# The last projection of a two-block transformer layer in seven half-size products instead of eight

## Chip, cores and metric

The kernel runs on one core of a Trainium2 chip. The metric is the device time of one execution in microseconds (us); the kernel is compared by the median of several executions. TensorE is called PE below, VectorE DVE, ScalarE ACT, GpSimd POOL, and SP is the queue that issues nearly all DMAs.

## What is computed

The reference is a sequence of two mixer blocks over 2048 tokens of width 1024, in float32. Only the end of the second block matters here:

```python
def swa_sink_mixer(xn, w_in, sinks, w_out, t5_table):
    q, k, v, z = split(xn @ w_in)
    o = banded_attention(q, k, v, t5_table, SWA_WINDOW, sinks)     # 16 heads, window 128
    return (merge_heads(o) * silu(z)) @ w_out                       # [2048,1024] @ [1024,1024]

x = x + swa_sink_mixer(rms_norm_2(x, norm_g), ...)
return rms_norm_2(x, final_g)
```

## The kernel before

The kernel is written as phases A, B1, B2, C, D and E, each a function that opens its own tile pools. Phase D computes the attention of the second block and stores its gated result, token tile by token tile, in DRAM as `y2[t]` (1024 x 128, already transposed for use as the stationary operand). Phase E, `phase_e`, is the last projection with the residual and the final norm: it loads `y2[t]` and `x2[t]` for each of 16 token tiles of 128, multiplies by `w_out`, adds the residual, and scales by the reciprocal root mean square and a gain.

Precision comes from splitting. Each float32 operand is cut into a high part (ACT copies it to the matmul type) and a low part (DVE or POOL subtracts the high part from the original), and `mm3` (L804 to L807) runs three matmuls for one 128-deep step: high by high, low by high, high by low. A token tile by half of the columns (512) is thus 8 steps of 3 matmuls; a token tile is 48 matmuls of 512 columns, and the phase 768 (the last tile's second half is cut in two, so 744 of 512 columns and 48 of 256).

A scheduler of the framework turns the program into one fixed order of instructions for each engine. Program order gives the priority; an instruction is placed once its inputs are there and its buffer is free, so a later phase may run in the gaps of an earlier one. Phase D's last stretch works in blocks `n` of one token tile and four heads: `scores(n)` (PE, then a fused add and max on DVE, L1115, then exponentials on ACT, L1120, and a scaling on POOL, L1128) and, two blocks later, `values(n-2)` (transposes, a high and low split on ACT and DVE, L1146 and L1147, matmuls, a copy on ACT, L1154, an addition on DVE, L1159, a product with the gate `e_z` on POOL, L1161, and the store to `y2`, L1162).

Memory decides when phase E may begin. Pools are laid out one behind another in the order in which they are opened. Phases D and E start from the same base, so each pool of E lies over certain pools of D. In KB per partition from that base, worked out from the shapes and buffer counts:

| pools of phase D | KB | pools of phase E before | KB |
|---|---|---|---|
| e_r (raw weights) | 0 to 8 | f_r | 0 to 4 |
| e_w0, e_w1 (split weights) | 8 to 40, 40 to 48 | f_w0, f_yr | 4 to 36, 36 to 40 |
| e_b (bias of the scores) | 48 to 56 | f_x0 | 40 to 48 |
| e_t (copies, outputs) | 56 to 63 | f_g (gain) | 48 to 52 |
| e_p (split probabilities) | 63 to 75 | f_x1 (7 buffers) | 52 to 80 |
| e_kv, e_s | 75 to 79.75 | f_s | 80 to 81.25 |
| e_a0, e_a1 (input x) | 79.75 to 131.75 | f_w1, f_y, f_j | 81.25 to 131.25 |
| e_q (queries) | 131.75 to 147.75 | f_x2 | 131.25 to 139.25 |
| e_z (gates), e_v (values) | 147.75 to 157.75, to 171.75 | | |
| e_k (keys), e_e (scores) | 171.75 to 187.75, to 203.75 | | |

In PSUM, phase D uses the eight banks as e_pm (0 to 2, projections), e_ps (3 and 4, scores), e_pt (5 and 6, transposes) and e_po (7, values). Phase E's one PSUM pool, `f_pm`, has three buffers and lies over e_pm. In the loop over tiles, `XN = 11` picks which of the three pools holds the tile of `x2`.

Of the kernel before, what the change touches and what calls it, by code (L numbers as in the profile page):

```python
# [7 lines left out]
F32 = mybir.dt.float32  # L8
F32R = mybir.dt.float32r
I32 = mybir.dt.int32  # L10
AF = mybir.ActivationFunctionType
ALU = mybir.AluOpType
AX = mybir.AxisListType
PSUM = bass.MemoryType.PSUM
DRAM = bass.MemoryType.DRAM

P = 128
S = 2048
D = 1024
NT = S // P  # L20
KD = D // P
# [782 lines left out]
def mm3(nc, ps, ah, al, bh, bl, first, last):  # L804
    nc.tensor.matmul(ps, ah, bh, start=first, stop=False)  # L805
    nc.tensor.matmul(ps, al, bh, start=False, stop=False)  # L806
    nc.tensor.matmul(ps, ah, bl, start=False, stop=last)  # L807
# [394 lines left out]
            pend = pend[per:]  # L1202


XN = 11


def phase_e(tc, c, scr, a_w_out, final_g, out):
    nc = tc.nc
    with (  # L1210
        tc.tile_pool(name="f_r", bufs=2) as rp,
        tc.tile_pool(name="f_w0", bufs=1) as wp0,
        tc.tile_pool(name="f_yr", bufs=1) as yrp,
        tc.tile_pool(name="f_x0", bufs=2) as xp0,
        tc.tile_pool(name="f_g", bufs=1) as gp,
        tc.tile_pool(name="f_x1", bufs=7) as xp1,
        tc.tile_pool(name="f_s", bufs=8) as sp,
        tc.tile_pool(name="f_w1", bufs=1) as wp1,
        tc.tile_pool(name="f_y", bufs=2) as yp,
        tc.tile_pool(name="f_j", bufs=1) as jp,  # L1220
        tc.tile_pool(name="f_x2", bufs=2) as xp2,
        tc.tile_pool(name="f_pm", bufs=3, space=PSUM) as pm,
    ):
        fg = gp.tile([P, D], F32, name="f_fg")
        nc.sync.dma_start(fg, final_g.unsqueeze(0).broadcast_to([P, D]))
        w = {}

        def load_w(ch, k):
            raw = rp.tile([P, 512], F32, name="f_raw")
            nc.sync.dma_start(raw, a_w_out[0, k * P:(k + 1) * P, ch * 512:(ch + 1) * 512])  # L1230
            t = (wp0, wp1)[ch].tile([P, 2, 512], F32R, name=f"f_w{ch}{k}")
            nc.scalar.activation(t[:, 0], raw, AF.Copy)
            nc.vector.tensor_sub(t[:, 1], raw, t[:, 0].bitcast(F32))
            w[ch, k] = t

        def load_y(t):
            yr = yrp.tile([P, KD, P], F32, name="f_yr")
            nc.sync.dma_start(yr, scr["y2"][t].rearrange("(k p) q -> p k q", p=P))
            y = yp.tile([P, 2, KD, P], F32R, name="f_y")
            nc.scalar.activation(y[:, 0], yr, AF.Copy)  # L1240
            nc.gpsimd.tensor_sub(y[:, 1], yr, y[:, 0].bitcast(F32))  # L1241
            return y

        ys = {0: load_y(0)}
        for ch in range(2):
            for k in range(KD):
                load_w(ch, k)
        for t in range(NT):
            if t + 1 < NT:
                ys[t + 1] = load_y(t + 1)  # L1250
            y = ys.pop(t)
            xt = (xp0, xp2, xp1)[min(t % XN // 2, 2)].tile([P, D], F32, name="f_xt")
            nc.sync.dma_start(xt, scr["x2"][t])  # L1253
            cuts = (0, 512, 1024) if t < NT - 1 else (0, 512, 768, 1024)
            sqs = []
            for a, b in zip(cuts, cuts[1:]):
                ch, ws = a // 512, slice(a % 512, a % 512 + b - a)
                ps = pm.tile([P, 512], F32, name="f_mm")[:, :b - a]
                for k in range(KD):
                    mm3(nc, ps, y[:, 0, k], y[:, 1, k], w[ch, k][:, 0, ws], w[ch, k][:, 1, ws], k == 0, k == KD - 1)  # L1260
                nc.vector.tensor_add(xt[:, a:b], ps, xt[:, a:b])  # L1261
                junk = jp.tile([P, 512], F32, name="f_j")
                sqs.append(sp.tile([P, 1], F32, name="f_sq"))
                nc.scalar.activation(junk[:, :b - a], xt[:, a:b], AF.Square, accum_out=sqs[-1])  # L1264
            ss = sqs[0]
            for sq in sqs[1:]:
                nc.vector.tensor_add(ss, ss, sq)
            rs = rsqrt_dve(nc, sp, ss, D)
            for a, b in ((0, D),) if t < NT - 1 else ((0, 512), (512, D)):
                nc.vector.scalar_tensor_tensor(xt[:, a:b], xt[:, a:b], rs, fg[:, a:b], ALU.mult, ALU.mult)  # L1270
                nc.sync.dma_start(out[0, t * P:(t + 1) * P, a:b], xt[:, a:b])


LAM_INIT = 0.8 - 0.6
# [101 lines left out]
```

## Time and profile before

| what | us |
|---|---|
| median of 3 runs | 3001.12 (2995.64 to 3003.31) |
| the profiled execution, its own time | 2997.43 |
| its span, first to last instruction | 2995.7 |

The span is the time from the first to the last instruction in the trace; the 1.7 us between it and the time lie around it. Times in the trace are counted from the span's start. A PE matmul of 512 columns shows 389 ns because matmuls are pipelined and overlap; the pace is read from starts, not from durations. A line number names the line of the kernel that issued an instruction.

### The profile page before, as it was taken

Reading aid. Unit: us, or ns where it says so; the run is one execution under the profiler, and the core shown is the slowest. Engines: PE = TensorE matmul, PEld = TensorE weight load, DVE = VectorE, ACT = ScalarE, POOL = GpSimd, SP = SyncE. Lnnn points to the kernel's source line nnn. Section 1 sums busy time; section 2 is a strip of 40 time slices with the busy share of each in tenths; the row PEclk is TensorE's granted clock in tenths of the full one; section 3 lists DMA queues with packets and bytes.
Section 4 is the critical chain, followed back from the end, with each engine's and each line's share of the span. In section 5 each row is a group of like instructions: output and inputs, shape, how many; then the busy total and the mean of one; then the engine's idle time right before and its main releaser. Section 6 shows DMA issues by size and latency. Waiting matters only on the chain. (4 is left out here: it accounts for less than half of the span.)

```text
span 2995.7 us, 45163 instructions
## 1 busy us (share of the span) xinstructions
PE 2893.5 (97%) x15554; PEld 2464.0 (82%) x15554; DVE 1802.1 (60%) x4607; ACT 1563.9 (52%) x3480; POOL 1240.7 (41%) x1156
## 2 busy tenths in 40 slices
PE   9999999999999999988898799999999999999998
PEld 7778888888788888888788678888788888888787
DVE  4115666522788889877666654444535756766765
ACT  5222333311588888878787642222345666666621
POOL 1110111100688888855676610000145565555421
PEclk9999999999999999999899999999999999999999
DMA  6653444414223322148666542332554343332452
GB/s 211 118 155 85 120 114 119 112 65 142 91 55 91 79 64 76 46 111 175 121 147 122 139 149 79 111 96 89 183 162 153 99 133 107 105 113 70 143 192 78
DMA packets 410646, 346.00 MB, mean 115 GB/s; under 512 B 89745, under 2 KB 356401, under 8 KB 408497
## 3 DMA queue, kind: packets, MB, share of 16 engines
q1 hardware_dynamic: 388000, 329.24, 39.3%
q10 hardware_dynamic: 20736, 8.65, 1.6%
q0 software_dynamic: 1680, 5.21, 0.7%
q8 instruction: 124, 2.03, 0.3%
q14 instruction: 106, 0.86, 0.1%
HBM read 227.51 MB, written 116.52 MB: 115 GB/s over the span
## 5 line engine op out<-in xcount | busy, mean ns | idle before, releaser
L190 PE MATMUL psm<-w,hh 128*128 128x512 f32 x1024 | 406.1, 398 | 9.4 <-DVE t L111 7.9
L191 PE MATMUL psm<-w,hl 128*128 128x512 f32 x1024 | 399.9, 392 | 0.0
L192 PE MATMUL psm<-w,hh 128*128 128x512 f32 x1024 | 399.8, 393 | 0.0
L101 POOL TENSOR_TENSOR w<-wraw,w 128x512 fp32r<-128x512 f32 x64 | 81.6, 1295 | 598.9 <-ACT w L100 596.3
L365 POOL TENSOR_TENSOR et<-et 128x1024 f32<-128x1024 f32 x124 | 296.3, 2414 | 0.0
L331 PE MATMUL s_ps<-kst,qst 128*128 128x512 f32 x1024 | 290.5, 408 | 4.1 <-DVE mx L337 3.1
L347 ACT ACTIVATE et<-et,nm 128x2048 f32<-128x2048 f32 x128 | 257.2, 2010 | 5.2
L1027 POOL TENSOR_TENSOR e_wt<-e_raw,e_wt 128x1024 fp32r<-128x1024 f32 x80 | 191.2, 2396 | 112.6 <-ACT e_wt L1026 111.4
L190 PEld LDWEIGHTS psm<-w,hh 128*128 128x128 f32 x1024 | 193.5, 189 | 48.1 <-DVE t L111 8.3
L805 PE MATMUL e_mm<-e_x,e_wt 128*128 128x512 f32 x576 | 228.1, 396 | 1.9 <-DVE e_k L1069 1.7
L807 PE MATMUL e_mm<-e_x,e_wt 128*128 128x512 f32 x576 | 226.8, 394 | 0.0
L192 PEld LDWEIGHTS psm<-w,hh 128*128 128x128 f32 x1024 | 193.2, 189 | 40.8
L806 PE MATMUL e_mm<-e_x,e_wt 128*128 128x512 f32 x576 | 226.6, 393 | 0.0
L191 PEld LDWEIGHTS psm<-w,hl 128*128 128x128 f32 x1024 | 193.7, 189 | 38.2
L331 PEld LDWEIGHTS s_ps<-kst,qst 128*128 128x128 f32 x1024 | 177.0, 191 | 43.7 <-DVE mx L337 17.3
L1128 POOL TENSOR_SCALAR e_es<-e_es,e_l 128x256 f32<-128x256 f32 (+1 forms) x256 | 118.8, 483 | 170.2 <-DVE e_l L1126 101.6
L364 POOL TENSOR_SCALAR et<-et,cc 128x1024 f32<-128x1024 f32 x124 | 138.3, 1132 | 110.4 <-PE psm L192 57.1
L377 DVE TENSOR_TENSOR ptl<-t_ps,pth 128x512 fp32r<-128x512 f32 x256 | 169.3, 684 | 18.9 <-ACT pth L376 18.4
L337 DVE CUSTOM_DVE_ANT_0 et<-s_ps,nd,mx 128x1024 f32<-128x1024 f32 x128 | 163.8, 1280 | 26.8 <-PE s_ps L331 24.9
L1115 DVE CUSTOM_DVE_ANT_0 e_es<-e_s,e_bias,e_sk 128x256 f32<-128x256 f32 (+1 forms) x256 | 117.3, 472 | 103.6 <-PE e_s L1107 72.1
L376 ACT ACTIVATE pth<-t_ps 128x512 fp32r<-128x512 f32 x256 | 143.6, 595 | 42.9 <-PE t_ps L375 38.9
L851 POOL TENSOR_TENSOR c_yn<-c_yn,ssq_sub 128x512 f32<-128x512 f32 x16 | 18.2, 1140 | 355.5 <-DMA c_yn<-s_y 327.5
(268 smaller groups left out, 7866.6 us busy)
## 6 DMA issues: line engine op xcount, KB each, us to landing
e_raw<-in_a_w_in_dram SPq DMA_DIRECT2D x80, 512.0 KB, 3.6
wraw<-in_w_in_dram SPq DMA_DIRECT2D x64, 256.0 KB, 3.5
kst<-s_dk SPq DMA_DIRECT2D x128, 128.0 KB, 3.9
s_xt<-c_at SPq DMA_DIRECT2D x32, 512.0 KB, 6.7
e_x<-s_xt SPq DMA_DIRECT2D x32, 512.0 KB, 7.9
t<-in_x_dram SPq DMA_DIRECT2D x32, 256.0 KB, 5.5
s_dv<-t SPq DMA_DIRECT2D x32, 256.0 KB, 3.0
s_bv<-t SPq DMA_DIRECT2D x32, 256.0 KB, 3.7
```

The lines of the kernel that those rows point to most:

```text
L190: nc.tensor.matmul(ps, ah, cur[k][:, 0], start=k == 0, stop=False)
L191: nc.tensor.matmul(ps, al, cur[k][:, 0], start=False, stop=False)
L192: nc.tensor.matmul(ps, ah, cur[k][:, 1], start=False, stop=k == KD - 1)
L331: nc.tensor.matmul(ps[:, b * 512:b * 512 + 512], lhs, heads[h, "k", e, i, 2 * hf + b], start=i == 0, stop=i == 1)
L337: nc.vector.tensor_tensor_reduce(et[:, hf], ps, bias[:, off:off + 1024], 1.0, -3.0e38 if hf == 0 else mx[:, 0:1], ALU.add, ALU.max, mx[:, ...
L347: nc.scalar.activation(ev, ev, AF.Exp, bias=nm, scale=slope, accum_out=st[g]["l"][:, e:e + 1])
L365: nc.gpsimd.tensor_sub(es[0][:, hf], es[0][:, hf], es[1][:, hf])
L377: nc.vector.tensor_sub(tl[:, :, qi], pt, th[:, :, qi].bitcast(F32))
L805: nc.tensor.matmul(ps, ah, bh, start=first, stop=False)
L806: nc.tensor.matmul(ps, al, bh, start=False, stop=False)
L807: nc.tensor.matmul(ps, ah, bl, start=False, stop=last)
L1027: nc.gpsimd.tensor_sub(w[:, 1], raw, w[:, 0].bitcast(F32))
```

## The change

`phase_e` is written anew. It takes two token tiles at once and cuts the product of the pair in two by two by two: two token tiles, two halves of the inner width (each 4 steps of 128), two halves of the columns. Eight half products become seven (Winograd's form of Strassen's scheme), each 4 steps of 3 matmuls of 512 columns, over these operands: a0 by w00, s2 by t2, s1 by t1, s3 by t3, s4 by w11, a1 by w10, b1 by t4. The weight combinations t1 to t4 are formed once (`weights`), the activation combinations s1 to s4 for each pair (`steps` in `load_pair`), each split anew into high and low. Seven weight operands of 4 tiles stand in place of 16 tiles. After each product its sum goes to the residual tiles `xa` and `xb` by way of a temporary `u` (ACT, DVE and POOL). The pools are new, too, in this order from the same base: `f_t` 0 to 32 KB (16 temporaries), `f_w0` 32 to 48 (w00), `f_x` 48 to 64 (x2), `f_g` 64 to 70, `f_s` 70 to 71.7, `f_w1` 71.7 to 135.7 (t1, t2, w10, t4), `f_y` 135.7 to 167.7 (8 split operands y), `f_w2` 167.7 to 199.7 (t3, w11). `f_pm` has seven PSUM buffers, banks 0 to 6. The last two tiles, not the last alone, are scaled and stored in halves. The new lines (removed ones, printed above, and empty ones are left out):

```diff
--- before.py
+++ after.py
@@ -1202,73 +1202,191 @@
             pend = pend[per:]
...
 def phase_e(tc, c, scr, a_w_out, final_g, out):
     nc = tc.nc
+    H = KD // 2
     with (
...
+        tc.tile_pool(name="f_t", bufs=TMP) as tp,
         tc.tile_pool(name="f_w0", bufs=1) as wp0,
...
+        tc.tile_pool(name="f_x", bufs=4) as xp,
         tc.tile_pool(name="f_g", bufs=1) as gp,
...
+        tc.tile_pool(name="f_s", bufs=6) as sp,
         tc.tile_pool(name="f_w1", bufs=1) as wp1,
...
+        tc.tile_pool(name="f_y", bufs=8) as yp,
+        tc.tile_pool(name="f_w2", bufs=1) as wp2,
+        tc.tile_pool(name="f_pm", bufs=7, space=PSUM) as pm,
     ):
+        def tmp():
+            return tp.tile([P, 512], F32, name="f_tmp", tag="f_tmp")
+        w = {}
+        def load_w(i, j, k):
+            raw = tmp()
+            nc.sync.dma_start(raw, a_w_out[0, (H * i + k) * P:(H * i + k + 1) * P, j * 512:(j + 1) * 512])
+            return raw
+        def split(key, k, raw, lo):
+            pool = wp0 if key == "w00" else wp2 if key in ("t3", "w11") else wp1
+            t = pool.tile([P, 2, 512], F32R, name=f"f_{key}_{k}")
+            nc.scalar.activation(t[:, 0], raw, AF.Copy)
+            lo.tensor_sub(t[:, 1], raw, t[:, 0].bitcast(F32))
+            w[key, k] = t
+        def weights():
+            ks = range(H)
+            w00 = [load_w(0, 0, k) for k in ks]
+            w01 = [load_w(0, 1, k) for k in ks]
+            for k in ks:
+                split("w00", k, w00[k], nc.vector)
+            for k in ks:
+                nc.gpsimd.tensor_sub(w00[k], w01[k], w00[k])
+            t1 = w00
+            w11 = [load_w(1, 1, k) for k in ks]
+            for k in ks:
+                split("t1", k, t1[k], nc.vector)
+            for k in ks:
+                nc.vector.tensor_sub(t1[k], w11[k], t1[k])
+                split("t2", k, t1[k], nc.vector)
+            t2 = t1
+            for k in ks:
+                nc.gpsimd.tensor_sub(w01[k], w11[k], w01[k])
+                split("t3", k, w01[k], nc.gpsimd if k % 2 else nc.vector)
+            for k in ks:
+                split("w11", k, w11[k], nc.gpsimd if k % 2 else nc.vector)
+            w10 = []
+            for k in ks:
+                w10.append(load_w(1, 0, k))
+                split("w10", k, w10[k], nc.gpsimd if k % 2 else nc.vector)
+            for k in ks:
+                nc.gpsimd.tensor_sub(t2[k], w10[k], t2[k])
+                split("t4", k, t2[k], nc.gpsimd if k % 2 else nc.vector)
+        ops, xs = {}, {}
+        def load_pair(n):
+            raw = {}
+            for i in range(2):
+                src = scr["y2"][2 * n + i].rearrange("(k p) q -> p k q", p=P)
+                for j in range(2):
+                    raw[i, j] = tmp()
+                    nc.sync.dma_start(raw[i, j].rearrange("p (k q) -> p k q", q=P), src[:, H * j:H * j + H])
+            def y_op(key, t, lo):
+                o = yp.tile([P, 2, H, P], F32R, name="f_y", tag="f_y")
+                tv = t.rearrange("p (k q) -> p k q", q=P)
+                nc.scalar.activation(o[:, 0], tv, AF.Copy)
+                lo.tensor_sub(o[:, 1], tv, o[:, 0].bitcast(F32))
+                ops[n, key] = o
+            def steps():
+                y_op("a0", raw[0, 0], nc.vector)
+                s1 = tmp()
+                nc.gpsimd.tensor_add(s1, raw[1, 0], raw[1, 1])
+                s2 = tmp()
+                nc.gpsimd.tensor_sub(s2, s1, raw[0, 0])
+                yield
+                y_op("s2", s2, nc.vector)
+                yield
+                y_op("s1", s1, nc.vector)
+                yield
+                nc.gpsimd.tensor_sub(raw[0, 0], raw[0, 0], raw[1, 0])
+                y_op("s3", raw[0, 0], nc.gpsimd)
+                yield
+                nc.gpsimd.tensor_sub(s2, raw[0, 1], s2)
+                y_op("s4", s2, nc.gpsimd)
+                yield
+                y_op("a1", raw[0, 1], nc.gpsimd)
+                yield
+                y_op("b1", raw[1, 1], nc.vector)
+                yield
+            xs[n] = []
+            for i in range(2):
+                xt = xp.tile([P, D], F32, name="f_xt")
+                nc.sync.dma_start(xt, scr["x2"][2 * n + i])
+                xs[n].append(xt)
+            return steps()
+        def product(n, ykey, wkey):
+            y = ops.pop((n, ykey))
+            ps = pm.tile([P, 512], F32, name="f_mm")
+            for k in range(H):
+                t = w[wkey, k]
+                mm3(nc, ps, y[:, 0, k], y[:, 1, k], t[:, 0], t[:, 1], k == 0, k == H - 1)
+            return ps
+        def add(x, j, ps):
+            nc.vector.tensor_add(x[:, 512 * j:512 * j + 512], ps, x[:, 512 * j:512 * j + 512])
+        def square(x, j, acc):
+            junk = gp.tile([P, 512], F32, name="f_j")
+            nc.scalar.activation(junk, x[:, 512 * j:512 * j + 512], AF.Square, accum_out=acc)
+        def finish(t, x, sq):
+            ss = sp.tile([P, 1], F32, name="f_ss")
+            nc.vector.tensor_scalar(ss, sq[0], sq[1], None, ALU.add)
+            rs = rsqrt_dve(nc, sp, ss, D)
+            for a, b in ((0, D),) if t < NT - 2 else ((0, 512), (512, D)):
+                nc.vector.scalar_tensor_tensor(x[:, a:b], x[:, a:b], rs, fg[:, a:b], ALU.mult, ALU.mult)
+                nc.sync.dma_start(out[0, t * P:(t + 1) * P, a:b], x[:, a:b])
+        first = load_pair(0)
+        for _ in range(2):
+            next(first)
+        weights()
+        for _ in first:
+            pass
         fg = gp.tile([P, D], F32, name="f_fg")
         nc.sync.dma_start(fg, final_g.unsqueeze(0).broadcast_to([P, D]))
...
+        for n in range(NT // 2):
+            nxt = load_pair(n + 1) if n + 1 < NT // 2 else iter(())
+            xa, xb = xs.pop(n)
+            sq = [[sp.tile([P, 1], F32, name=f"f_sq{i}{j}") for j in range(2)] for i in range(2)]
+            p = product(n, "a0", "w00")
+            u = tmp()
+            nc.scalar.activation(u, p, AF.Copy)
+            nc.gpsimd.tensor_add(xa[:, 0:512], xa[:, 0:512], u)
+            next(nxt, None)
+            p = product(n, "s2", "t2")
+            nc.vector.tensor_add(u, p, u)
+            nc.gpsimd.tensor_add(xa[:, 512:D], xa[:, 512:D], u)
+            next(nxt, None)
+            p = product(n, "s1", "t1")
+            add(xa, 1, p)
+            add(xb, 1, p)
+            next(nxt, None)
+            p = product(n, "s3", "t3")
+            nc.vector.tensor_add(u, p, u)
+            for j in range(2):
+                nc.gpsimd.tensor_add(xb[:, 512 * j:512 * j + 512], xb[:, 512 * j:512 * j + 512], u)
+            next(nxt, None)
+            p = product(n, "s4", "w11")
+            add(xa, 1, p)
+            square(xa, 1, sq[0][1])
+            square(xb, 1, sq[1][1])
+            next(nxt, None)
+            p = product(n, "a1", "w10")
+            add(xa, 0, p)
+            square(xa, 0, sq[0][0])
+            finish(2 * n, xa, sq[0])
+            next(nxt, None)
+            p = product(n, "b1", "t4")
+            add(xb, 0, p)
+            square(xb, 0, sq[1][0])
+            for _ in nxt:
+                pass
+            finish(2 * n + 1, xb, sq[1])
+TMP = 16
 LAM_INIT = 0.8 - 0.6
```

## Rows read from the trace of the kernel before

**Rows 1.** The page: busy time, share of the span and instructions of each engine.

```profile
PE 2893.5 (97%) x15554; PEld 2464.0 (82%) x15554; DVE 1802.1 (60%) x4607; ACT 1563.9 (52%) x3480; POOL 1240.7 (41%) x1156
```

**Rows 2.** Busy time by stretch: length, engines, granted clock, DMA share, GB/s.

```profile
2780.00:2794.00 14.00, 10.88 (x55) 8.93 (x54) 10.03 (x33) 10.53 (x29) 5.47 (x7) 0.88 0.76 230
2794.00:2858.00 64.00, 63.32 (x318) 52.25 (x318) 52.76 (x142) 37.53 (x96) 30.70 (x44) 1.00 0.49 156
2858.00:2988.00 130.00, 129.46 (x593) 107.70 (x591) 73.06 (x170) 28.29 (x63) 26.33 (x11) 1.00 0.38 131
```

**Rows 3.** Tile f_mm, 2788 to 2857.6 us: durations ns min/median/max, first and last start.

```profile
L805 PE MATMUL f_mm<-f_w,f_y x67: 389/389/500, 2794.4 to 2857.5; 128*128 128x512 f32 x67
```

**Rows 4.** SP's queue in order of time: start, us, line and DMA.

```profile
2779.76 0.36 SPq L1238 DMA_DIRECT2D f_yr<-s_y  x1
...
2830.01 0.96 SPq L1253 DMA_DIRECT2D f_xt<-s_x  x2
2831.46 0.33 SPq L1225 DMA_DIRECT2D f_fg<-in_final_g_dram  x1
...
2857.57 0.37 SPq L1162 DMA_DIRECT2D s_y<-e_o  x1
2858.70 5.20 SPq L1253 DMA_DIRECT2D f_xt<-s_x  x8
...
2914.76 0.37 SPq L1238 DMA_DIRECT2D f_yr<-s_y  x1
...
2925.64 0.37 SPq L1238 DMA_DIRECT2D f_yr<-s_y  x1
```

**Rows 5.** Timeline of DVE and POOL, apart: last reads of phase D's pools.

```profile
2830.95 0.48 DVE L1115 CUSTOM_DVE_ANT_0 e_es<-e_s,e_bias,e_sk 128x256 f32<-128x256 f32 x1
...
2846.95 1.29 DVE L1147 TENSOR_TENSOR e_pl<-e_tp,e_ph 128x512 fp32r<-128x512 f32 x2
...
2856.67 0.88 POOL L1161 TENSOR_TENSOR e_o<-e_o,e_z 128x128 f32<-128x128 f32 x2 [4.44 <-DVE e_o L1159]
```

**Rows 6.** Groups by line and shape, 2779.7 to 2857.6 us: count, busy us, mean ns, idle before.

```profile
L1233 DVE TENSOR_TENSOR f_w<-f_raw,f_w 128x512 fp32r<-128x512 f32 x16 | 12.9, 817 | 2.4 <-ACT f_w L1232 2.2
L1115 DVE CUSTOM_DVE_ANT_0 e_es<-e_s,e_bias,e_sk 128x256 f32<-128x256 f32 x26 | 12.1, 476 | 3.9 <-PE e_s L1107 3.7
L1147 DVE TENSOR_TENSOR e_pl<-e_tp,e_ph 128x512 fp32r<-128x512 f32 x16 | 10.6, 684 | 0.3 <-ACT e_ph L1146 0.2
L1232 ACT ACTIVATE f_w<-f_raw 128x512 fp32r<-128x512 f32 x16 | 10.0, 628 | 9.1 <-DMA f_raw<-in_a_w_out_dram 7.1 <-issue 2.0
L1159 DVE TENSOR_TENSOR e_o<-e_o,e_tmpb 64x256 f32<-64x256 f32 x18 | 7.5, 414 | 1.8 <-ACT e_tmpb L1154 1.0 <-issue 0.7
```

**Rows 7.** Timeline of DVE and PE where no f_mm has begun.

```profile
2787.57 0.47 DVE L1115 CUSTOM_DVE_ANT_0 e_es<-e_s,e_bias,e_sk 128x256 f32<-128x256 f32 x1
...
2792.14 0.47 DVE L1115 CUSTOM_DVE_ANT_0 e_es<-e_s,e_bias,e_sk 128x256 f32<-128x256 f32 x1
...
2788.10 0.90 PE L1107 MATMUL e_s<-e_k,e_q 128*128 128x256 f32 x4 [2.64 <-DVE e_mx L1115]
```

**Rows 8.** Groups by line and shape, 2600 us to the end.

```profile
L1241 POOL TENSOR_TENSOR f_y<-f_yr,f_y 128x1024 fp32r<-128x1024 f32 x16 | 38.3, 2392 | 96.9 <-ACT f_y L1240 90.9 <-DVE e_mx L1115 6.1
L1261 DVE TENSOR_TENSOR f_xt<-f_mm,f_xt 128x512 f32<-128x512 f32 x31 | 21.0, 687 | 29.2 <-PE f_mm L807 28.7 <-DMA f_xt<-s_x 0.3
L1264 ACT ACTIVATE f_j<-f_xt 128x512 f32<-128x512 f32 x31 | 19.4, 625 | 78.2 <-DVE f_xt L1261 42.1 <-issue 29.6 <-DMA f_xt<-s_x 6.5
L1270 DVE SCALAR_TENSOR_TENSOR f_xt<-f_xt,rd_y,f_fg 128x1024 f32<-128x1024 f32 x15 | 19.3, 1285 | 2.7 <-DMA f_fg<-in_final_g_dram 2.2
```

**Rows 9.** Busy time by stretch, just after that idle time of PE.

```profile
2792.00:2796.00 4.00, 4.00 (x21) 3.57 (x20) 2.99 (x12) 3.95 (x11) 0.00 (x0) 0.76 0.25 74
```

**Rows 10.** Timeline of the end, from the last matmul.

```profile
2987.30 0.28 PE L807 MATMUL f_mm<-f_w,f_y 128*128 128x256 f32 x1
2987.62 0.42 DVE L1261 TENSOR_TENSOR f_xt<-f_mm,f_xt 128x256 f32<-128x256 f32 x1 [1.65 <-PE f_mm L807]
```

More of the change, by code (lines that the diff above doesn't have):

```diff
@@ L1202, in phase_d @@
             pend = pend[per:]
-XN = 11
 def phase_e(tc, c, scr, a_w_out, final_g, out):
     nc = tc.nc
+    H = KD // 2
     with (
-        tc.tile_pool(name="f_r", bufs=2) as rp,
+        tc.tile_pool(name="f_t", bufs=TMP) as tp,
         tc.tile_pool(name="f_w0", bufs=1) as wp0,
-        tc.tile_pool(name="f_yr", bufs=1) as yrp,
-        tc.tile_pool(name="f_x0", bufs=2) as xp0,
+        tc.tile_pool(name="f_x", bufs=4) as xp,
         tc.tile_pool(name="f_g", bufs=1) as gp,
-        tc.tile_pool(name="f_x1", bufs=7) as xp1,
-        tc.tile_pool(name="f_s", bufs=8) as sp,
+        tc.tile_pool(name="f_s", bufs=6) as sp,
@@ L1218, in phase_e @@
         tc.tile_pool(name="f_w1", bufs=1) as wp1,
[L1219 to L1222, printed above, removed]
-    ):
+        tc.tile_pool(name="f_y", bufs=8) as yp,
+        tc.tile_pool(name="f_w2", bufs=1) as wp2,
+        tc.tile_pool(name="f_pm", bufs=7, space=PSUM) as pm,
+    ):
+        def tmp():
[105 more added lines that the diff above has]
+            pass
@@ L1224, in phase_e @@
         fg = gp.tile([P, D], F32, name="f_fg")
         nc.sync.dma_start(fg, final_g.unsqueeze(0).broadcast_to([P, D]))
[L1226 to L1271, printed above, removed]
```

## The prediction

> **What bounds the kernel now.** I read the page first: PE is busy for 97% of the span and no other engine comes near [rows 1]. Then the stretches around phase E. From 2794 to 2988 us PE has no room: 63.3 of 64 us, then 129.5 of 130 [rows 2]. But these are two kinds of stretch. In the first, phase D still runs: its last product with the gate ends at 2857.55 [rows 5]. PE is full there only because matmuls of phase E fill the gaps: by 2857.5 it has run 199 of E's 792 (the row of one line, x67, stands; those of the two others have x66 each) [rows 3]. In the second PE runs phase E alone, one token tile every 10.88 us [rows 4], or 10.88 / 48 = 0.2267 us a matmul. So the 199 were worth 45.1 us of PE time that cost nothing. The last matmul ends at 2987.58 [rows 10], and 8.1 us later the span.
>
> The question is thus double: how many matmuls fewer, and how many can still run under D's tail. For the second I read SP's queue, since a DMA into a pool shows when the pool opens. The gain `f_fg` lies over the first half of e_b, and is issued at 2831.46, when the last read of any bias ends (2830.95 + 0.48) [rows 4, 5]. f_x1 lies over e_b to e_a0, and its first buffer (52 to 56 KB) over e_b's second half alone, free since 2831.4. Yet nothing is loaded into any of its seven buffers until the batch of eight loads at 2858.70, behind the last product on POOL and the last store from e_t [rows 4, 5]. So a pool waits for every pool under any part of it; no buffer opens by itself. f_yr opens at 2779.76 [rows 4], and f_mm, over e_pm alone, starts at 2794.4 [rows 3].
>
> **When the new pools open.** Laid against the table: f_t lies over e_r and e_w0 and opens at about 2780; f_w0 over e_w0 and e_w1, soon after. So raw loads, w00's split, s1, s2, and t1's and part of t3's raw differences can run under D. Nothing else can. f_pm with seven banks lies over the transposes, read last by L1147 at 2848.2 [rows 5]. f_w1 begins at 71.7 KB, inside e_p (63 to 75), and f_w2 lies over e_v, e_k and e_e: all these live until D's last matmuls. f_y lies over e_q, e_z and e_v, and e_z is read by the very last product, so it opens latest; f_x waits for e_t besides. Call the end of that last product T1. No matmul of phase E starts before T1: all 45.1 us of cover are gone.
>
> **What that does to T1.** With PE's gaps unfilled, D's tail can run faster. DVE's main work of D left at 2780 is 12.1 + 10.6 + 7.5 = 30.2 us [rows 6], and w00 adds 4 x 0.82 = 3.3. That puts T1 at 2814 at the earliest, and with the short operations and the last block's chain at 2820. The other bound is 2857.6, as before. Where no f_mm had begun, six heads of scores took 5 us, 2787.57 to 2792.61 [rows 7]; all 26 from 2780 to 2831.4 took 51 us [rows 5, 6], 2 us each against 0.84. So the tail is held by PE's order, not by DVE, and I take a value nearer the low end. Nine blocks of values are left (L1159 x18) [rows 6]; at 6 us each T1 = 2834. PE may run this at the lower clock: after 2.64 us of idle time the granted clock was 0.76 from 2792 to 2796 [rows 7, 9]; that is why I don't take 5 us a block.
>
> **The sum after T1.** First matmul: ACT's copy of a0 (0.63 [rows 6]), DVE's subtraction (0.7 to 0.8) and the hand-overs, 2.2 us. Matmuls: 7 x 12 x 8 = 672 at 0.2267 = 152.3 us. Before it was 45.1 + 130.0 = 175.1, so the scheme does save 22.8.
>
> Stalls of the first pair. A POOL subtraction of 512 columns is half of L1241's 2.39, 1.2 us [rows 8]. From about T1 - 2.9, when f_w1 and f_w2 open, POOL has 2 differences of t3, 8 low parts, 4 differences of t4 and 5 operations for s3, s4 and a1: 19 x 1.2 = 22.8 us. The 16 temporaries are all taken then (4 raw y, s1, s2, 4 of t1, 4 of w01, 2 of w11), so w11's last two and w10's four loads wait for one to be freed, and POOL waits for them, some 5 us in all. POOL would be through the pair at T1 + 25, and two products of 2.7 us still follow: T1 + 30, against T1 + 2.2 + 19.0 = 21.2 without stalls. The next pair waits 1 us more. Bounds: 0, if the scheduler puts s4 and a1 into POOL's early gaps, and 15, if DVE's list (20 weight operations, 4 low parts, 7 sums from PSUM, 20 us) comes on top in part. I take 9.5, as the list of POOL gives it. PE starts from little work, so 1.5 us for the lower clock [rows 9].
>
> Steady state costs nothing more. A pair is 84 matmuls, 19.0 us of PE. POOL has 11 operations, 13.2 us. DVE has 7 sums at 0.69, 4 low parts at 0.82, 2 scalings at 1.29 [rows 6, 8] and two chains of short operations under 3 us each, 16 us. ACT has 8 copies and 4 squares at 0.63, under 9. Each operand is made a pair ahead. If a pair took 1 us more on DVE, the cover would be gone and it would cost 7 us.
>
> Tail: 8.1 us before. The last sum and square are of 512 columns in place of 256, 0.5 more, and tile 14's finish, one product earlier, stands in front of them on DVE: 0 to 3 us, I take 0.9. So 9.5.
>
> Sum: 2834 + 2.2 + 152.3 + 9.5 + 1.5 + 9.5 = 3009.0. With the 1.7 us around the span 3010.7, against the profiled execution's 2997.43: 13.3 us slower. The median of the runs shown is 3.7 above that execution, so I add the difference to the median: 3014.
>
> **Rivals.** (a) D's tail shrinks to DVE's floor: T1 = 2820, and 14 us less, about 3000, no change. For it speak the six heads in 5 us; against it the chain of one block through five engines, and the lower clock. (b) The other side, faster: buffers open one by one and not with their pool. Then PSUM banks 0 to 2 are free at 2794, the products start under D as before, and the 22.8 us are kept less 1.4 of tail: 2980. It decides where the 45 us of cover are kept; for it only that f_mm starts early before, against it the eight loads at 2858.70 and f_fg. (c) D's tail does not shrink: T1 = 2857.6, 3038. Against it rows 7. (d) POOL and DVE shut each other out: a subtraction with both inputs in SBUF took 817 ns on the mean while POOL worked, one with PSUM 684 [rows 6]. If each of DVE's 24 such operations in the first pair blocked POOL for 0.69 us, POOL's 23 operations up to its last sum, 27.6 us, became 44, and the pair ended 10 us later: 3024. The rows show only 0.13 us each. The Trainium skill (SBUF — State Buffer, "Who interferes with whom") has a rule for this: a DVE operation with two SBUF inputs and a POOL operation that reads SBUF exclude each other for a whole instruction. By that rule the sum would be 3024; by the rows, 3014.
>
> **From these to the numbers.** 0.3%, 9 us, is about what a measurement of this kernel can tell from no change. The forecast has 0.57, with 3005 to 3023 as its own range, a sixth of it within 9 us of 3001; (a) 0.20; (b) 0.07; (c) 0.06; (d) 0.10. Slower: 0.57 x 5/6 + 0.06 + 0.10 and a little of (a), 0.65; same 0.28; faster (b), 0.07. The range leaves out (b), most of (c) and the corner of (a) with no stalls: 2997 to 3033.
>
> **What would show it.** The first f_mm starts 1 to 3 us after the last L1161 product of D, not near 2794, and PE is mostly idle from 2795 to T1. Loads into the `f_x` tiles come right after the last store to y2, in a batch. D's last product ends at 2826 to 2845. The first 84 f_mm take 25 to 33 us, with waits on POOL; later pairs 19.0 each. The prediction is wrong if f_mm start while D's scores run, if T1 is below 2822, or if the steady pair is not 19 us.

## The result: slower by 1.4%

The kernel with seven products takes 3040.36 us (median of 4, 3038.2 to 3043.81), the kernel before in the same rounds 3000.7: a ratio of 1.014, 95% interval 1.0126 to 1.0155, or 40 us slower. The prediction said 3014 and a range up to 3033: its direction came, its size did not. The profiled execution took 3042.17 us, its span 3040.4.

The page of the changed kernel, busy time and then the chain that ended last, by engine. PE's share has fallen from 97% to 95% [rows 1]; its busy time has not (2896.1 us against 2893.5), although it has 120 matmuls fewer. The largest part of the chain that ends last is DVE's.

```profile
PE 2896.1 (95%) x15434; PEld 2458.2 (81%) x15434; DVE 1870.5 (62%) x4670; ACT 1590.6 (52%) x3538; POOL 1354.9 (45%) x1248
...
DVE 4%; issue 1%; POOL 1%; DMA 1%; PE 0%; ACT 0%; POOLq 0%; DVEq 0%; SPq 0%; ACTq 0%
```

Where phase E begins: the last product of phase D on POOL, SP's queue around it, and two rows of the tile `f_mm` (first and last start of its matmuls).

```profile
2830.86 1.76 POOL L1161 TENSOR_TENSOR e_o<-e_o,e_z 128x128 f32<-128x128 f32 x2 [2.06 <-issue]
```

```profile
2829.28 0.42 SPq L1348 DMA_DIRECT2D f_fg<-in_final_g_dram  x1
2832.65 0.36 SPq L1162 DMA_DIRECT2D s_y<-e_o  x1
2834.58 1.28 SPq L1314 DMA_DIRECT2D f_xt<-s_x  x3
```

```profile
L805 PE MATMUL f_mm<-f_w,f_y x96: 387/389/796, 2834.5 to 3017.8; 128*128 128x512 f32 x96
...
L807 PE MATMUL f_mm<-f_t,f_y x128: 387/389/794, 2844.1 to 3021.0; 128*128 128x512 f32 x128
```

The product ends at 2832.6 (T1). Before, `f_mm` started at 2794.4, under phase D [rows 3]; now its first matmul comes at 2834.5, 1.9 us behind T1, and the `x2` loads come in a batch behind the last store. So far all is as predicted, but for one sign: PE is not mostly idle from 2795 to T1. From there the windows tell the rest (length, busy time of PE, PEld, DVE, ACT and POOL with counts, granted clock, DMA share, GB/s):

```profile
2844.50:2854.50 10.00, 6.51 (x26) 4.56 (x24) 10.00 (x7) 6.32 (x13) 10.00 (x7) 0.95 0.49 151
...
2894.50:2914.50 20.00, 20.00 (x90) 16.48 (x89) 18.87 (x37) 6.17 (x15) 14.62 (x10) 1.00 0.48 159
...
2954.50:2974.50 20.00, 17.56 (x78) 14.21 (x77) 15.19 (x34) 6.36 (x15) 13.93 (x10) 1.00 0.50 159
2974.50:2994.50 20.00, 17.11 (x68) 13.59 (x67) 15.21 (x27) 6.31 (x14) 14.01 (x11) 0.91 0.44 144
...
3021.20:3040.40 19.20, 0.21 (x1) 0.00 (x0) 12.65 (x34) 2.89 (x8) 3.72 (x3) 0.58 0.22 83
```

The first line is the one to read: DVE and POOL are both busy for all of 10 us, and each gets only seven operations done. Later PE is full for three pairs, then runs dry again, with DVE at 15 and POOL at 14 of 20 us. The last matmul ends at 3021.2 (its start at 3021.0 and the pace of 0.23), so the matmuls take 186.7 us from first to last, where 672 at 0.2267 are 152.3. Then come 19.2 us without PE, where before had 8.1 [rows 10]. Counted by the starts of its matmuls, 84 at a time, the 186.7 us are 32.6, 30.4, 19.1, 19.1, 19.1, 21.8, 23.9 and 20.6: the loss lies in the first two blocks and in the last three. (A block is not quite a pair: PE runs 12 matmuls of the second pair before the first pair's last, which ends at 2870.4.)

Why seven operations take 10 us is seen in the timelines of the two engines, DVE first, then POOL (start, us, operations merged by line):

```profile
2849.70 1.75 DVE L1240 TENSOR_TENSOR f_w<-f_tmp,f_w 128x512 fp32r<-128x512 f32 x1
2851.38 5.12 DVE L1240 TENSOR_TENSOR f_t<-f_tmp,f_t 128x512 fp32r<-128x512 f32 x3
2856.42 3.46 DVE L1240 TENSOR_TENSOR f_w<-f_tmp,f_w 128x512 fp32r<-128x512 f32 x2
```

```profile
2850.86 1.73 POOL L1240 TENSOR_TENSOR f_w<-f_tmp,f_w 128x512 fp32r<-128x512 f32 x1
2852.55 5.08 POOL L1269 TENSOR_TENSOR f_tmp<-f_tmp 128x512 f32<-128x512 f32 x3
2857.59 1.75 POOL L1240 TENSOR_TENSOR f_w<-f_tmp,f_w 128x512 fp32r<-128x512 f32 x1
```

Each engine finishes one subtraction every 1.7 us, in step with the other. An earlier one on DVE, at 2837.68, when POOL stood idle, took 0.68, and POOL's of this size take 1.26 to 1.31 alone. One behind the other they would take some 1.96 us, side by side 1.28: at 1.71 the two come near to taking turns. This is called the lock below. The turns need not be even. Here one low part on DVE lasts 5.46 us, while POOL runs four operations without a gap, and PE waits 5 us for it (timelines of DVE, POOL and PE):

```profile
2873.59 5.46 DVE L1286 TENSOR_TENSOR f_y<-f_tmp,f_y 128x512 fp32r<-128x512 f32 x1
```

```profile
2873.57 1.28 POOL L1292 TENSOR_TENSOR f_tmp<-f_tmp 128x512 f32<-128x512 f32 x1
2874.79 1.27 POOL L1300 TENSOR_TENSOR f_tmp<-f_tmp 128x512 f32<-128x512 f32 x1
2876.01 2.49 POOL L1369 TENSOR_TENSOR f_xt<-f_xt,f_tmp 128x512 f32<-128x512 f32 x2
```

```profile
2879.11 0.79 PE L806 MATMUL f_mm<-f_t,f_y 128*128 128x512 f32 x1 [4.99 <-DVE f_y L1286]
```

In the later pairs (groups of DVE, 2885 to 3021 us; count, busy us, mean ns, idle before):

```profile
L1338 DVE SCALAR_TENSOR_TENSOR f_xt<-f_xt,rd_y,f_fg 128x1024 f32<-128x1024 f32 x13 | 28.7, 2204 | 0.2
L1286 DVE TENSOR_TENSOR f_y<-f_tmp,f_y 128x512 fp32r<-128x512 f32 x25 | 27.7, 1124 | 21.0 <-ACT f_y L1285 21.0
L1327 DVE TENSOR_TENSOR f_xt<-f_mm,f_xt 128x512 f32<-128x512 f32 x30 | 19.5, 678 | 0.3 <-issue 0.3
```

The scaling, 1285 ns in before [rows 8], takes 2204; the low parts take 1124; the sums with one input in PSUM take 678 (687 before [rows 8]). The waits of 2880 to 3021 us, longest first in total, show the second half of it:

```profile
ACT f_y L1285 <- POOL f_tmp L1300: 30.7, 6, 7.3
DVE f_y L1286 <- ACT f_y L1285: 21.0, 6, 4.5
...
PE f_mm L806 <- DVE f_y L1286: 6.5, 3, 2.9
```

ACT stands behind a late POOL, DVE behind ACT, PE behind DVE: so DVE has idle time and is late all the same. By these waits alone POOL could be slow on its own account; the experiments e9 and e11 decide that.

### The profile page after: what moved, and what is told of

Read it like the earlier page. It is cut to its first block, busy times and chain, and to the rows that moved or that the text cites. A ratio compares the mean times of both kernels' runs of the same rounds, so it can differ in the third digit from the quotient of the medians.

```text
span 3040.4 us, 45276 instructions
## 1 busy us (share of the span) xinstructions
PE 2896.1 (95%) x15434; PEld 2458.2 (81%) x15434; DVE 1870.5 (62%) x4670; ACT 1590.6 (52%) x3538; POOL 1354.9 (45%) x1248
```

## The experiments

Phases ahead of E end up to 16 us apart from run to run (the last bias load is issued at 2764.1 before, 2766.1 after and up to 2779.7 below), and chips differ; each run below is compared with runs of the kernel before on its own chip, and terms are counted from T1 or the first `f_mm`. "Stretch" is first start to last end of `f_mm`, "tail" what follows.

**e1_before_7banks**: the kernel before, but no bank of `f_pm` is free under D's tail.

```diff
-        tc.tile_pool(name="f_pm", bufs=3, space=PSUM) as pm,
+        tc.tile_pool(name="f_pm", bufs=7, space=PSUM) as pm,
```

> The kernel before with one number changed: seven PSUM buffers in the pool of the last projection in place of three, so that it lies over the banks of the scores and the transposes too. Theory (a pool opens as a whole, when every pool under it is done): no matmul of the last projection starts at 2794 us any more; the first starts when the last transposed tile is read, some 2828 to 2835 us, D's tail ends near 2833 as in the changed kernel, and as weights and y are ready the 792 matmuls follow without a gap: 2830 + 175 + 8, a span of 3010 to 3016 us, 13 to 18 us slower than before. Rival (a buffer opens by itself, and the stalls of the changed kernel alone make it slow): first matmul near 2794 us and no change.

Measured: 3030.35 against 3008.26, ratio 1.007 (1.0055 to 1.0085), 22 us slower. T1 2849.9, first `f_mm` 2847.1, behind the last transposes; window of the stretch:

```profile
2847.00:3023.20 176.20, 176.20 (x793) 146.57 (x792) 95.53 (x215) 36.83 (x79) 34.41 (x16) 0.99 0.35 121
```

PE runs its 792 matmuls without a gap, all but the first 2.8 us of them behind D. So the loss of cover alone costs 22 us (13 to 18 were expected): about half of the 45 us that the matmuls are worth, since D's tail gets shorter: T1 comes 70.2 us behind the last bias load, where before it was 93.4.

**e2_waits_by_tile**: each of the nine pools declared with waits by tile.

```diff
-        tc.tile_pool(name="f_t", bufs=TMP) as tp,
+        tc.tile_pool(name="f_t", bufs=TMP, reuse_waits="tile") as tp,
...
```

> The changed kernel, with its nine pools told to wait buffer by buffer for what lies under each, and not as whole pools. Theory: PSUM banks 0 to 2 and some y buffers open under D's tail, so the first matmul of the projection starts between 2795 and 2815 us in place of 2834.5; but t1's first tile and t3's tiles still lie under buffers that D reads to its end, so only two to four products gain cover: 5 to 12 us faster than the changed kernel, 3028 to 3035 us. Rival (the start does not matter, the list of DVE and POOL does): within 4 us of 3040.

Measured: 3044.41, ratio 1.0125 (1.0108 to 1.0143). The option left the order of instructions on every engine as it was; the first `f_mm` came at 2839.4, 1.9 us behind T1 (2837.5). The expected gain is not there, and the run tells nothing of the theory.

**e3_weights_on_dve**: the 20 weight operations of POOL given to DVE.

```diff
-                split("t3", k, w01[k], nc.gpsimd if k % 2 else nc.vector)
+                split("t3", k, w01[k], nc.vector)
...
```

> The changed kernel, with the 20 POOL operations that form and split the weights moved to DVE. Theory (a DVE operation with two SBUF inputs and a POOL operation shut each other out: both ran at one per 1.71 us together from 2841 to 2865 us, against 0.6 to 0.69 and 1.28 alone): a weight operation costs DVE 0.6 to 0.7 us when POOL is quiet, the 1.71 us rhythm disappears for most of the start-up, and the first pair is through 8 to 14 us earlier: 3026 to 3033 us. Rival (DVE's list is simply long; its operations are slow for another reason): DVE's list grows from 24 to 44 operations and the first pair ends up to 10 us later, 3040 to 3050 us.

Measured: 3042.25 against 3008.26, ratio 1.011 (1.0095 to 1.0125). Stretch 177.0 us against 186.7, tail 17.5. DVE has 20 operations more and PE is 9.7 us earlier through, which speaks for the lock and against DVE's mere load. The gain is not where it was expected: the first 84 matmuls take 29.5 us for 32.6, the second 84 take 19.1 for 30.4, and later blocks lose some of it again (21.8, 23.9, 20.6 and 23.9 us among the last five).

**e4_direct_last_pair**: the last pair's sums go straight from PSUM into the residual.

```diff
+            last = n == NT // 2 - 1
...
+            if last:
+                for x in (xa, xb):
+                    for j in range(2):
+                        add(x, j, p)
...
```

> The changed kernel; in the last pair alone every product is added from PSUM straight to the residual tiles on DVE (14 additions), with no temporary u, no ACT copy and no POOL addition. Theory (the 19 us from the last matmul to the end are the chain of u through ACT, DVE and POOL): 11 to 13 us from the last matmul to the end, 6 to 8 us faster, about 3033 us. Rival (DVE is late with older work, the norm and scaling of the pair before): the end stays 17 to 20 us behind the last matmul, 3040 us, or more as DVE has 7 more operations.

Measured: 3049.6, ratio 1.0137 (1.0122 to 1.0152); stretch 186.3, tail 19.8. The chain through `u`, ACT and POOL is not what makes the tail long. That theory falls; the rival, older work on DVE, fits.

**e5_after_again**: the changed kernel once more, beside the next three.

> The changed kernel itself once more, as the base for the next three on one chip. Every theory: ratio to before 1.013 to 1.015, some 40 us slower; matmuls of phase E last 185 to 189 us and the tail behind them 18 to 20 us.

Measured: 3047.84 against 3005.61, ratio 1.0139 (1.0122 to 1.0157). Stretch 187.2, tail 16.3 (18 to 20 was expected; so the tail of one and the same kernel differs by 3 us between two profiles).

**e6_three_banks**: the changed kernel with three PSUM buffers in `f_pm`.

```diff
-        tc.tile_pool(name="f_pm", bufs=7, space=PSUM) as pm,
+        tc.tile_pool(name="f_pm", bufs=3, space=PSUM) as pm,
```

> f_pm has 3 PSUM buffers instead of 7. Theory (DVE is the bound of phase E, and PE only runs ahead of it by as many sums as there are buffers): the end stays within 4 us of the changed kernel, the matmul stretch grows by 6 to 12 us and the tail behind the last matmul shrinks by as much, to 8 to 13 us. Rival 1 (the tail of 19 us is a chain of its own, of norm, scaling and store): the tail stays at 17 to 20 us and the total grows by what PE waits more, 6 to 12 us. Rival 2 (PE's run-ahead is what keeps the pace): the stretch grows by 20 us or more.

Measured: 3050.07, ratio 1.0145 (1.0128 to 1.0162), 2 us over e5. Stretch 195.8, tail 10.4. Against e5 the tail loses 5.9 us and the stretch gains 8.6; PE's new wait is for the sums:

```profile
PE f_mm L805 <- DVE f_xt L1327: 12.2, 6, 3.1
```

So the long tail is not work at the end. It is lag: seven banks let PE run ahead of sums that are late anyway.

**e7_no_pool**: all of phase E's POOL work given to DVE.

```diff
-                nc.gpsimd.tensor_sub(w00[k], w01[k], w00[k])
+                nc.vector.tensor_sub(w00[k], w01[k], w00[k])
...
-                y_op("s3", raw[0, 0], nc.gpsimd)
+                y_op("s3", raw[0, 0], nc.vector)
...
-            nc.gpsimd.tensor_add(xa[:, 0:512], xa[:, 0:512], u)
+            nc.vector.tensor_add(xa[:, 0:512], xa[:, 0:512], u)
...
```

> All of phase E's POOL work is given to DVE: the weight operations and, in each pair, 4 combinations, 3 low parts and 4 additions into the residual. Theory (DVE's operations with two SBUF inputs and POOL's shut each other out): the 512-column operations on DVE fall to 0.60 to 0.70 us each from 1.1 to 1.7, the scaling of 1024 to 1.29 from 2.20, and DVE's list of a pair is 7 x 0.69 + 4 x 0.62 + 7 x 0.68 + 4 x 0.62 + 2 x 1.29 + short operations = 18 to 19.5 us, under PE's 19.0 or just at it: the matmul stretch shrinks from 187 to 160 to 172 us, the tail to 9 to 15 us, the total by 15 to 30 us. Rival (the loss is DVE's load as such, and POOL carries a real share of it): DVE has 11 more operations, 7 us, in each pair of 22 us, so the stretch grows by 10 to 40 us and the total with it.

Measured: 3017.62 against 3005.61, ratio 1.0043 (1.0026 to 1.0059): 30 us faster than e5. T1 2840.9, first `f_mm` 2842.8, stretch 162.8, tail 10.4. Groups of DVE, 2880 to 3000 us, and two windows:

```profile
L1286 DVE TENSOR_TENSOR f_y<-f_tmp,f_y 128x512 fp32r<-128x512 f32 x44 | 29.9, 696 | 2.5 <-ACT f_y L1285 2.5
...
L1338 DVE SCALAR_TENSOR_TENSOR f_xt<-f_xt,rd_y,f_fg 128x1024 f32<-128x1024 f32 x12 | 15.3, 1280 | 0.0
```

```profile
2862.80:2872.80 10.00, 7.80 (x34) 5.71 (x32) 10.00 (x17) 3.42 (x6) 0.00 (x0) 1.00 0.33 98
...
2942.80:2962.80 20.00, 19.92 (x88) 16.18 (x87) 18.87 (x37) 7.38 (x16) 0.00 (x0) 1.00 0.81 263
```

One engine does the work of two in less time: 17 operations in 10 us where DVE and POOL together had 14. In the later pairs PE is nearly full and DVE just fits, 18.87 of 20 us; the first two blocks of 84 matmuls take 24.0 and 22.0 us, the others 19.1 to 20.9.

**e8_no_scaling**: the scaling of the output left out.

```diff
-                nc.vector.scalar_tensor_tensor(x[:, a:b], x[:, a:b], rs, fg[:, a:b], ALU.mult, ALU.mult)
```

> Leaves out the final scaling of the output (the norm's factor and the gain are computed and loaded, but the residual sum is stored unscaled); POOL's work stays. Takes 2.2 us twice in each pair from DVE, 4.4 of 22 us. Theory (DVE, slowed by POOL, is the bound of the later pairs): they run at PE's pace of 19.0 to 19.7 us, the stalls behind the first pair go (8 us), the lag of the sums goes with them and the tail shrinks by 6 to 10 us, of which 2.8 are the scalings of the last pair themselves: the total falls by 12 to 20 us. Rival (the later stalls come from the order of waits between ACT, POOL and DVE and not from DVE's load): only the end's own scalings are gained, 3 to 5 us.

Measured: 3031.41 against 3005.61, ratio 1.0085 (1.007 to 1.01), 16 us under e5. Stretch 174.2, tail 8.3. Taking work from DVE does help, and by more than the scalings of the last pair, so the lateness of DVE sets the pace: the last six blocks of 84 matmuls take 19.1 us each. Whether it is DVE's time that is won or POOL's is not told apart, since a scaling has two SBUF inputs and holds POOL up too. The stalls of the first 40 us stay (PE 30.6 of 40).

**e9_idle_pool_work**: e7, with POOL working on what nobody waits for.

```diff
+                for _ in range(2 if key in ("s3", "s4", "a1", "b1") else 1):
+                    nc.gpsimd.tensor_sub(z, o[:, 0].bitcast(F32), o[:, 1].bitcast(F32))
                 ops[n, key] = o
```

> The kernel with all work on DVE, and POOL given work that nobody waits for: 11 subtractions of 512 columns in each pair, which read the split operands and write one scratch tile. Theory (the engines shut each other out, so the price is in DVE's own durations): DVE's operations with two SBUF inputs go back to 1.0 to 1.7 us wherever POOL works, those with a PSUM input stay at 0.68; the stretch and tail together grow by 20 to 60 us over the 173 us without POOL work. Rival (POOL was only a slow link in the chain of operands, 1.3 to 2 us for each hand-over, and DVE's durations did not matter): POOL is in no chain here, so the total stays within 3 us of the kernel without POOL work.

Measured: 3089.49 against 3009.1, ratio 1.0267 (1.0251 to 1.0284): 68 us more than e7 loses to its own base, from work whose results nobody uses (POOL ends only 1.7 us of the other engines' waits from 2845 to 3078 us). Stretch and tail together grow by 70 us over e7, more than the 20 to 60 expected. Groups of DVE and of POOL, 2880 to 3000 us, and a window:

```profile
L1288 DVE TENSOR_TENSOR f_y<-f_tmp,f_y 128x512 fp32r<-128x512 f32 x33 | 34.9, 1074 | 0.0
...
L1331 DVE TENSOR_TENSOR f_xt<-f_mm,f_xt 128x512 f32<-128x512 f32 x20 | 13.0, 675 | 0.0
```

```profile
L1290 POOL TENSOR_TENSOR f_z<-f_y 128x512 f32<-128x512 f32 x53 | 90.4, 1706 | 36.5 <-DVE f_y L1288 24.3 <-DVE rd_i L249 3.7 <-DVE rd_v L247 3.4
```

```profile
2905.30:2985.30 80.00, 56.34 (x228) 45.10 (x227) 80.00 (x137) 23.11 (x51) 55.61 (x35) 0.85 0.27 86
```

DVE shows as busy for 80 of 80 us, and PE, with operands late, falls to 56. The low parts went from 696 to 1074 ns, the sums from PSUM stayed at 675 (690 in e7). So POOL need not be in any chain to do the harm.

**e10_early_pools**: e7 with `f_y` and t1 laid over phase D's projections, three PSUM banks in a pool of their own, and the second and third product exchanged.

```diff
+        tc.tile_pool(name="f_w2a", bufs=1) as wp2a,
+        tc.tile_pool(name="f_y", bufs=8) as yp,
+        tc.tile_pool(name="f_wt1", bufs=1) as wpt,
         tc.tile_pool(name="f_w1", bufs=1) as wp1,
...
+        tc.tile_pool(name="f_pm", bufs=3, space=PSUM) as pm,
+        tc.tile_pool(name="f_pn", bufs=4, space=PSUM) as pn,
```

> The kernel with all work on DVE, and its pools laid out anew so that two of the first pair's seven products (a0 by w00, s1 by t1) need only pools over phase D's projections: f_y and t1 at 80 to 128 KB, three PSUM banks in a pool of their own over e_pm. Theory (cover under D's tail is worth its matmuls and the operands' preparation): the first f_mm starts near 2800 instead of T1 + 2, 24 matmuls (5.4 us) and some 15 DVE operations of the first pair run under D, the stretch behind T1 shrinks from 165 to 150 to 158 us, and the total falls by 6 to 16 us: within 6 us of the kernel before on either side. Rival (the work put early delays D's own tail by what it gains): T1 is 8 us or more later and the total within 3 us of the kernel without POOL work.

Measured: 3020.45 against 3009.1, ratio 1.0042 (1.0029 to 1.0054): as e7. The first `f_mm` starts at 2802.8 and 152 us of stretch are left behind T1, but T1 itself comes at 2856.3, 82.5 us behind the last bias load where e7 has 69.9. The window shows who is full there:

```profile
2814.00:2824.00 10.00, 5.60 (x19) 4.13 (x17) 9.96 (x23) 3.40 (x11) 5.41 (x5) 0.55 0.34 118
```

From 2804 to 2834 DVE is busy for 29.3 of 30 us. The rival holds: T1 is later by as much as was gained. DVE has little room under D's tail, and what phase E does there earlier, D does later.

**e11_second_input_in_psum**: POOL's work as in the changed kernel; DVE's second input moved to PSUM.

```diff
+            ps = hp.tile([P, 512], F32, name="f_hi", tag="f_hi")
+            nc.scalar.activation(ps, hi.bitcast(F32), AF.Copy)
...
-                lo.tensor_sub(o[:, 1], tv, o[:, 0].bitcast(F32))
+                lo.tensor_sub(o[:, 1], tv, high(o[:, 0], lo))
...
-                nc.vector.scalar_tensor_tensor(x[:, a:b], x[:, a:b], rs, fg[:, a:b], ALU.mult, ALU.mult)
+                nc.vector.scalar_tensor_tensor(x[:, a:b], x[:, a:b], rs, pg[j], ALU.mult, ALU.mult)
```

> The changed kernel with POOL's work as it was, but DVE's low parts (all but w00's) read the high part from a PSUM copy that ACT writes besides (0.6 us each), and the scaling reads the gain from PSUM, in two halves; f_pm has 4 banks to make room. DVE's operations of 512 columns thus have one SBUF input. Theory (the exclusion needs two SBUF inputs on DVE): low parts on DVE take 0.68 to 0.75 us and a half of the scaling 0.68 to 0.75, although POOL works beside them; POOL's take 1.28 to 1.35; the total falls 12 to 30 us below the changed kernel's 3041 to 3048. Rival (any DVE operation on SBUF data slows beside POOL, or ACT's 40 to 60 added copies cost as much): low parts stay over 1.0 us, or the total falls by less than 6 us.

Measured: 3024.2 against 3007.86, ratio 1.0046 (1.003 to 1.0061). Stretch 169.9, tail 10.0. Groups of DVE, then of POOL, 2885 to 3010 us:

```profile
L1349 DVE SCALAR_TENSOR_TENSOR f_xt<-f_xt,rd_y,f_pg 128x512 f32<-128x512 f32 x28 | 19.6, 742 | 0.2
L1297 DVE TENSOR_TENSOR f_y<-f_tmp,f_hi 128x512 fp32r<-128x512 f32 x25 | 16.6, 682 | 3.5 <-ACT f_hi L1239 3.5
```

```profile
L1311 POOL TENSOR_TENSOR f_tmp<-f_tmp 128x512 f32<-128x512 f32 x6 | 7.8, 1292 | 0.3 <-DVE rd_y L251 0.3
```

The same line in the changed kernel, 2885 to 3021 us, and a window of e11:

```profile
L1300 POOL TENSOR_TENSOR f_tmp<-f_tmp 128x512 f32<-128x512 f32 x6 | 12.0, 2007 | 1.1 <-DVE rd_i L249 1.1
```

```profile
2878.90:3012.90 134.00, 134.00 (x589) 110.17 (x587) 98.01 (x261) 65.93 (x137) 94.25 (x75) 1.00 0.41 136
```

POOL has the same work as in the changed kernel, and both engines run at their own speed: 682 and 742 ns on DVE, 1292 on POOL for 2007. The first 84 matmuls take 36.0 us; from there on PE is never idle, at 19.1 us for 84, though POOL is busy 94 of 134 us and operands still pass through it. That settles the mechanism for the later pairs: two SBUF inputs on DVE, not POOL's work or its hand-overs as such. The four PSUM buffers are not the reason, as e6 with three gained nothing in the total.

**e12_psum_and_pool_sums**: e11 with all low parts on DVE (`nc.gpsimd` to `nc.vector` in the seven calls of `split` and `y_op` that had it); t1's and t2's low parts read SBUF alone again.

> As the one before, and all low parts are DVE's; POOL keeps the combinations s1 to s4 and t1, t3, t4 and the additions into the residual (8 operations a pair, 10.3 us at 1.28). t1's and t2's low parts read SBUF alone. If the exclusion is gone from the pairs, DVE has 7 x 0.69 + 7 x 0.68 + 4 x 0.69 + short operations 3 = 15.5 us a pair: PE is the bound, the pairs take 19.0 us, the total is 3012 to 3022 on this chip, 2 to 6 us under the kernel without POOL work if the first pair's stalls shrink. Rival (POOL's slow hand-overs to ACT and DVE are what costs then): the later pairs take over 20 us and the total is over 3025.

Measured: 3035.03 against 3007.86, ratio 1.0086 (1.0071 to 1.0101). The theory's 3012 to 3022 is missed. Durations are clean (684 ns on DVE in the pairs, 1.29 to 1.30 us on POOL), yet the stretch is 180.7. A window of the later pairs, PE's longest wait of 2842 to 2890 us, and the copy that it waits for:

```profile
2886.90:3023.50 136.60, 136.60 (x601) 112.40 (x599) 108.83 (x280) 75.00 (x153) 64.79 (x51) 1.00 0.42 135
```

```profile
PE f_mm L805 <- ACT f_tmp L1372: 10.7, 1, 10.7
```

```profile
2868.05 0.60 ACT L1372 ACTIVATE f_tmp<-f_mm 128x512 f32<-128x512 f32 x1
```

The theory holds for the later pairs: after the first 84 matmuls they take 19.1 us each, and PE is never idle. The rival, later pairs of over 20 us, falls. The loss is all in the first 84 matmuls, 46.7 us for 24.0 in e7. There PE has filled its four PSUM buffers and needs the first of them back; ACT empties it only at 2868.05, 16 us after the last matmul into it, behind its copies of the weights. So what fails is the start in this form. Whether more PSUM buffers or an earlier copy would mend it was not tried and stays open.

## Why the prediction was right in its direction and wrong in its size

**Right: when phase E may begin.** T1 was put at 2834 and came at 2832.6; the first matmul at T1 + 2.2 came at T1 + 1.9. No `f_mm` ran under D. e1 shows the step by itself: without cover the old scheme loses 22 us. Rivals (a), (b) and (c) did not happen. The number is in part luck: it rests on 6 us for a block of phase D, a choice between two bounds, and the sign that was to go with it did not come. PE was not mostly idle under D's tail but busy for 27.1 of 37.6 us, at a granted clock of 0.77 on the mean:

```profile
2795.00:2832.60 37.60, 27.13 (x123) 20.74 (x121) 31.14 (x92) 26.77 (x75) 27.04 (x46) 0.77 0.23 78
```

**Wrong: the stalls of the first pair, 9.5 us, and "steady state costs nothing more".** Matmuls with stalls and clock were put at 152.3 + 9.5 + 1.5 = 163.3 us and took 186.7, 23.4 more: about 14 in the first two blocks of 84 matmuls (63.0 us for 2 x 19.0 + 9.5 + 1.5) and 9.5 in the other six, where the sum has none. The first block itself, 32.6 us, is within the sign of 25 to 33, but the first pair's last matmul came at T1 + 37.8 and not T1 + 30. The step that failed is the choice in rival (d): the sum priced DVE's and POOL's operations as if each had its engine's time for itself, because the rows showed 817 against 684 ns, 0.13 us each [rows 6]. That mean was taken where POOL was busy 30.7 of 64 us [rows 2], and 11 of its 16 operations took 0.68 to 0.71 us. The price stood in single rows of the same trace (timelines of DVE and POOL before):

```profile
2800.67 1.89 DVE L1233 TENSOR_TENSOR f_w<-f_raw,f_w 128x512 fp32r<-128x512 f32 x1 [0.71 <-ACT f_w L1232]
```

```profile
2799.63 2.39 POOL L1241 TENSOR_TENSOR f_y<-f_yr,f_y 128x1024 fp32r<-128x1024 f32 x1
```

With POOL busy all the time the same kind of operation took 1.7 us. The Trainium skill (SBUF — State Buffer, "Who interferes with whom") has the rule that the prediction weighed and set aside: a DVE operation with two SBUF inputs and a POOL operation that reads SBUF exclude each other for whole instructions. Here the trace agrees with it in the main, 1.71 us each in step where strict turns would be 1.96, and so does e11, where one input in PSUM frees both engines. By that rule the prediction named 3024: it priced the first pair alone, ending 10 us later than in the sum (it was 7.8), and left out that in the later pairs a scaling takes 2204 ns for 1285 and a low part 1124 for 696 (e7).

**Wrong: the tail, 9.5 us, came at 19.2.** It is not a longer chain at the end (e4) but the same lateness, carried to the end by PE's seven banks (e6). In e7 and e11, where the sums are in time, it is 10.4 and 10.0.

**Without POOL's work the total is the predicted one, partly by luck.** In e7 stretch and tail are 162.8 + 10.4 = 173.2 us; predicted were 163.3 + 9.5 = 172.8. Its distance from the kernel before is 12.0 us, the prediction's 13.3. But the 9.5 us of stalls in the sum were worked out from POOL's list, and e7 has no such list; its 10.5 us over 152.3 have another source, and what of them is the lower clock and what DVE's list was not separated. The books close all the same: 22 us of lost cover (e1), 22.8 saved by fewer matmuls (the prediction's 175.1 - 152.3), 10.5 of stalls, 2.3 more of tail, together the 12.0 of e7, and 30 for POOL's work (e5 minus e7): 42, against the 40 to 42 measured.

How much of the 30 us is the lock is settled for the later pairs alone: there e11 leaves POOL its work, frees DVE's second input, and PE runs without a gap. At the start it is not settled. The first two blocks of 84 matmuls take 63.0 us in the changed kernel, 55.1 in e11, 65.8 in e12, 48.6 in e3 and 46.0 in e7, so that order and hand-overs of the first operands count there too, by shares that no run tells apart. In the total e11 gets back 0.93% of 1.39%, e7 0.96%.

No version here beats the kernel before. The best, e7, e10 and e11, are 0.4 to 0.5% slower and cannot be told apart, and e10 says why cover does not come back: DVE is nearly full under D's tail.

## What to carry to other kernels

Before moving work to POOL to relieve DVE, count how many of DVE's operations beside it have both inputs in SBUF: here their times nearly added instead of overlapping. And do not take the price from a mean over a stretch in which POOL works half of the time; look for single operations beside a POOL operation. A second input in PSUM, or no POOL at all, was faster here than two engines taking turns. When fewer matmuls are bought with more elementwise work, and with pools that open later, price the cover lost and the engine that then becomes full, not the matmuls alone; and read a tail behind a deep PSUM queue as lag of earlier work.

## What the runs showed of the hardware that was not expected

Even an operation on one column is held up. In the tail of the changed kernel (timeline of DVE, then of POOL), a product of two 128x1 tiles, 0.15 us in other places of the same timeline, takes 1.26 beside a POOL addition that starts 0.01 us earlier and takes 1.26:

```profile
3021.18 1.26 DVE L265 TENSOR_TENSOR rd_y<-rd_y,rd_a 128x1 f32<-128x1 f32 x1
```

```profile
3021.17 1.26 POOL L1360 TENSOR_TENSOR f_xt<-f_xt,f_tmp 128x512 f32<-128x512 f32 x1 [3.14 <-DVE rd_a L264]
```

So short chains of such operations, as the one for the norm's factor, can pay nearly a whole POOL instruction for one step; on the mean of the later pairs L265 took 597 ns, and 155 in e7, without POOL's work. Operations with one tensor input were not touched: L257, a scalar operation on 128x1, kept 0.27 us throughout.
